# Whole-piece hi/lo splits, paired accumulator banks, and a fourth seven-product piece in every second gate-and-up loop

## The chip, the cores and the metric

The kernel runs on one core of one Trainium2 chip. The metric is the device time of one execution in microseconds (us); 1098.47 us is the median of three runs of the kernel before (1098.34 to 1099.88). Engines are named as in the profile: PE (TensorE matmul), PEld (its weight load), DVE (VectorE), ACT (ScalarE), POOL (GpSimd), SP (SyncE, which issues the weight loads).

## The reference, cut to what matters

One decoder layer on 256 tokens of width 2048, in float32. The two mixers in its first half are left out here, since the change doesn't touch them:

```python
h = _rms(x, norm1_g)
proj = einsum('bsd,de->bse', h, w_in)              # 2048 -> 6144
...                                                # gated MLP heads and retention heads
x = x + einsum('bse,ed->bsd', mixed, w_out)        # 2048 -> 2048
h2 = _rms(x, norm2_g)
a = silu(einsum('bsd,df->bsf', h2, w_gate)) * einsum('bsd,df->bsf', h2, w_up)   # 2048 -> 5632
x = x + einsum('bsf,fd->bsd', a, w_down)           # 5632 -> 2048
return _rms(x, final_norm_g)
```

## The kernel before

**Numbers.** Every operand of a product is split into a high and a low part, `hi` (a rounded copy, made by ACT in L54) and `lo` (the rest, source minus `hi`, made by DVE in L55). A product is three matmuls of 128x512 columns: hi by hi, hi by lo, lo by hi (`three`, `mm` in L46). Weights come from memory by SP in pieces of 128x2048 (`raw`, three buffers). `hi` and `lo` have four buffers each of 128x1024, so that a piece takes two of each, and a buffer comes free when the last matmul that reads it has ended.

**Stages.** `gemm_tok` runs the products with w_in (12 of them) and w_out (4); each has four pieces. Then come 11 loops over w_gu (`j` in 0 to 10, 512 columns of gate and 512 of up in each) and two halves over w_down (`c` in 0 and 1, 22 pieces each). These last two stages are written by `quad`.

**Pieces of `quad`.** A w_gu loop has 8 pieces, 0 to 7. One piece is a 2x2 product of blocks: token halves by inner halves, and inner halves by column halves. A *classic* piece makes its 8 block products in 24 matmuls. A *seven* makes them in seven products, 21 matmuls, by Strassen's way with fewer sums (Winograd's form): DVE first makes four sums of weight blocks in a tile `t` (L499, 128x1024, and L502 and L503, 128x512 each), and splits three stretches of `raw` as well as the four of `t`. `SEVEN_GU = (1, 3, 5)` says which pieces are sevens in each loop; in w_down these are 2, 6, 10, 14 and 17.

**Accumulators.** PSUM has four banks of `acc` for the results 11, 12, 21 and 22 and four of `sm`, which a quad uses for products 1, 5, 7 and 6. After the last seven of a quad ACT copies product 1 (L549) and DVE makes four mixes of the others (L550 to L553). These stand in a tile `mT2` or `mT3` until `finish_up`, where after the last piece DVE adds each of the four acc banks to its mix (L599, L600, 128x512, twice each), ACT makes silu (`sg`, L604) and DVE the product (L605), for each token half. The next loop's first matmuls reuse the acc banks that these adds read. `turn_a` transposes the product of loop j by 8 PE transposes (L615) in loop j+1, ahead of its piece 6, and ACT copies them out (L616).

**Order.** Each engine works through its own queue in the order in which the built program has it, and nothing overtakes. That order is set by a scheduler at build time, from the program's text and its buffers; it is shown below where it matters.

**The end.** In the second half over w_down the last two pieces are kept (`apart`) and run bank by bank: 11, 12, 21, 22, 12 matmuls each. DVE adds each bank to `x` in two steps of 256 columns (L684), ACT sums the squares (L226), a chain of small DVE steps makes the row's norm (L91 to L79), and DVE and ACT scale the row (L697, L700, L702) before it is stored.

## Time and profile before

| | |
|---|---|
| median of three runs | 1098.47 us |
| profiled execution | 1098.69 us |
| its span, first to last instruction | 1096.9 us |
| mean granted TensorE clock | 0.996 |
| PE busy | 1081.2 us, 99% of the span |
| PEld busy | 894.3 us, 82% |
| DVE busy | 863.4 us, 79% |
| ACT busy | 602.3 us, 55% |
| POOL busy | 26.2 us, 2% |

The share is busy time over the span. "Start us" in a timeline is counted from the span's start; the second number is how long one record, or a run of neighbours (x2, x3), took. Two instructions of one engine that follow each other overlap a little in the records, so the pace of an engine is read from one start to the next, and not from the recorded length.

### The profile page before, as it was taken

The page shows a single profiled execution, that of the slowest core. Times are in us where ns is not written, and L with a number is a line of the kernel's source. Part 1 is how long each engine was busy: PE and PEld are TensorE (multiplying, and loading weights), DVE is VectorE, ACT ScalarE, POOL GpSimd, SP SyncE. Part 2 cuts the span into 40 slices and gives each one's busy share as a digit, 9 for nine tenths or more (in the row PEclk, how much of TensorE's full clock was granted, in tenths as well). Part 3 has the DMA queues.
Part 4 walks back from the last instruction along what each step waited for, and adds up shares of the span by engine and source line. Part 5 has one row for each costly group of instructions (what it writes and reads, how often), then busy time and mean ns, then how long its engine had stood idle before and what let it go on. Part 6 is the DMA issues. An engine that isn't in the chain of part 4 may idle for free.

```text
span 1096.9 us, 12958 instructions
## 1 busy us (share of the span) xinstructions
PE 1081.2 (99%) x4907; PEld 894.3 (82%) x4907; DVE 863.4 (79%) x1149; ACT 602.3 (55%) x744; POOL 26.2 (2%) x20
## 2 busy tenths in 40 slices
PE   8999999999999999999999999999999999999996
PEld 7878888888888888888888888888888888888884
DVE  6786457466546799898898898898899887998786
ACT  6563435444445556555555655656566656565463
POOL 0110011000000000000000000000000000020000
PEclk9999999999999999999999999999999999999998
DMA  9855544445555455645655555556556655646552
GB/s 344 340 211 194 189 171 170 176 156 189 192 192 187 164 186 192 230 172 189 220 187 192 206 196 213 192 192 220 173 191 222 231 192 192 215 169 230 192 192 77
DMA packets 32750, 217.65 MB, mean 198 GB/s; under 512 B 3760, under 2 KB 4144, under 8 KB 7088
## 3 DMA queue, kind: packets, MB, share of 16 engines
q1 hardware_dynamic: 32544, 215.78, 54.9%
q0 software_dynamic: 144, 1.05, 0.3%
q8 instruction: 38, 0.62, 0.2%
q14 instruction: 24, 0.20, 0.1%
HBM read 214.72 MB, written 2.10 MB: 198 GB/s over the span
## 4 chain that ended last, share of the span: by engine, by line
PE 97%; DVE 1%; DMA 1%; ACT 0%; SPq 0%; issue 0%; DVEq 0%; ACTq 0%
PE acc L46 83%; PE sm L46 12%; PE sm L615 1%; DMA raw<-in_w_in 1%; PE sm L454 0%; PE sm L346 0%; PE sm L395 0%; DVE x L697 0%; ACT junk L226 0%; DVE x L684 0%; SPq L176 0%; DVE rs_w L78 0%; DVE st L258 0%; ACT hi L54 0%; SPq L173 0%
## 5 line engine op out<-in xcount | busy, mean ns | idle before, releaser
L46 PE MATMUL acc<-hi,hT 128*128 128x512 f32 x2364 | 752.1, 391 | 3.4 <-ACT hi L54 3.4
L54 ACT CAST hi<-raw 128x1024 fp32r<-128x1024 f32 (+1 forms) x396 | 387.9, 997 | 385.5 <-PE acc L46 358.8
L55 DVE TENSOR_TENSOR lo<-raw,hi 128x1024 fp32r<-128x1024 f32 (+1 forms) x396 | 453.0, 1161 | 181.3 <-ACT hi L54 180.0
L46 PEld LDWEIGHTS acc<-hi,hT 128*128 128x128 f32 x2364 | 443.8, 188 | 95.8 <-ACT hi L54 5.0
L46 PE MATMUL acc<-lo,hT 128*128 128x512 f32 x1182 | 460.8, 390 | 0.7 <-DVE lo L55 0.7
L46 PEld LDWEIGHTS acc<-lo,hT 128*128 128x128 f32 x1182 | 222.0, 188 | 48.3 <-DVE lo L55 3.6
L55 DVE TENSOR_TENSOR lo<-mT,hi 128x1024 fp32r<-128x1024 f32 x86 | 105.0, 1221 | 24.5 <-ACT hi L54 24.5
L54 ACT CAST hi<-mT 128x1024 fp32r<-128x1024 f32 x86 | 90.7, 1055 | 40.9 <-DVE lo L55 21.4
L46 PE MATMUL sm<-hi,h2s 128*128 128x512 f32 x258 | 93.5, 389 | 0.0
L46 PE MATMUL acc<-hi,mT 128*128 128x512 f32 x256 | 80.1, 391 | 0.0
L46 PEld LDWEIGHTS sm<-hi,h2s 128*128 128x128 f32 x258 | 48.4, 188 | 10.0
L46 PEld LDWEIGHTS acc<-hi,mT 128*128 128x128 f32 x256 | 48.1, 188 | 10.3 <-ACT mT L398 0.5
L499 DVE TENSOR_TENSOR mT<-raw 128x1024 f32<-128x1024 f32 x43 | 52.5, 1220 | 1.3 <-DMA raw<-in_w_gu 0.6
L46 PE MATMUL sm<-lo,h2s 128*128 128x512 f32 x129 | 50.2, 389 | 0.0
L46 PE MATMUL acc<-lo,mT 128*128 128x512 f32 x128 | 49.7, 389 | 0.0
L46 PE MATMUL sm<-hi,hT 128*128 128x512 f32 x86 | 33.5, 389 | 0.0
L46 PE MATMUL acc<-hi,h2s 128*128 128x512 f32 x86 | 33.5, 389 | 0.0
L502 DVE TENSOR_TENSOR mT<-raw,mT 128x512 f32<-128x512 f32 x43 | 30.6, 711 | 0.0
L604 ACT ACTIVATE sg<-mT,rstd 128x512 f32<-128x512 f32 x22 | 15.9, 722 | 24.7 <-DVE mT L599 24.7
L503 DVE TENSOR_TENSOR mT<-raw,mT 128x512 f32<-128x512 f32 x43 | 29.4, 684 | 0.0
L46 PEld LDWEIGHTS sm<-lo,h2s 128*128 128x128 f32 x129 | 24.2, 188 | 5.0
L46 PEld LDWEIGHTS acc<-lo,mT 128*128 128x128 f32 x128 | 24.0, 188 | 4.8
(111 smaller groups left out, 564.5 us busy)
## 6 DMA issues: line engine op xcount, KB each, us to landing
raw<-in_w_gu SPq DMA_DIRECT2D x88, 1024.0 KB, 4.7
raw<-in_w_in SPq DMA_DIRECT2D x47, 1024.0 KB, 4.8
raw<-in_w_down SPq DMA_DIRECT2D x44, 1024.0 KB, 4.7
raw<-in_w_out SPq DMA_DIRECT2D x16, 1024.0 KB, 4.7
x<-in_x SPq DMA_DIRECT2D x2, 1024.0 KB, 8.8
gains<-in_gains SPq DMA_DIRECT2D x2, 1024.0 KB, 6.2
out<-x SPq DMA_DIRECT2D x8, 256.0 KB, 2.5
work<-in_xT SPq DMA_DIRECT2D x7, 256.0 KB, 8.7
```

What stands on the lines that cost most here:

```text
L46: nc.tensor.matmul(o, lhsT=l, rhs=r, start=start, stop=stop)
L54: nc.scalar.copy(hi, src[:, c:c + step])
L55: nc.vector.tensor_tensor(out=lo, in0=src[:, c:c + step], in1=hi.bitcast(F32), op=ALU.subtract)
L499: nc.vector.tensor_tensor(out=t13.rearrange("p (b c) -> p b c", b=2), in0=b12.unsqueeze(1).broadcast_to([P, 2, NC]), in1=raw[:, NC:3 * NC] ...
L502: nc.vector.tensor_tensor(out=t24[:, 0:NC], in0=b22, in1=t13[:, 0:NC], op=ALU.subtract)
L503: nc.vector.tensor_tensor(out=t24[:, NC:], in0=b21, in1=t24[:, 0:NC], op=ALU.subtract)
L604: nc.scalar.activation(sg, g, AF.Silu, scale=rstd2[r])
L615: nc.tensor.transpose(ps[:, q * S + n * P:q * S + (n + 1) * P], rows[n][:, f * P:(f + 1) * P], ident)
```

## The change

1. `hi` and `lo`: three buffers of 128x2048 instead of four of 128x1024. A classic piece of `quad` is split by one ACT copy and one DVE subtraction of 2048 columns (new lines L53 and L54), where there were two of 1024. A seven's splits become two, 1536 columns of `raw` and 2048 of `t`, where there were four. `gemm_tok` still splits in steps of 1024, now into halves of one buffer.
2. `acc`: two tiles of two banks each (11 with 12, 21 with 22). `finish_up` adds a pair in one instruction of 1024 columns (L605, two in a loop, for the four L599 and L600). A pair is free for the next quad when its one add has read it.
3. Sevens of w_gu: pieces 0, 2, 4 and 6 in loops with odd `j` (five loops), 2, 4 and 6 in loops with even `j` (six). The last seven is now piece 6, so that the mixes (L555 to L558) stand after piece 6, and one classic piece is left behind it; it was piece 5, with two behind it. Products run in the order 1, 3, 2, 5, 7, 6, 4.
4. `turn_a` stands ahead of piece 7 (was 6); in loop 0 the last turn of x and the norm stand ahead of piece 1 (was 5).
5. The scratch tiles `sums` and `hf` now share the two buffers of `sg`; the load of the final gains `gf` moves from POOL's queue to SP's, in the first half over w_down.

```diff
-SEVEN_GU = (1, 3, 5)
+SEVEN_GU = (0, 2, 4, 6)
...
-    acc = ctx.enter_context(tc.tile_pool(name="acc", bufs=4, space=PSUM))
+    acc = ctx.enter_context(tc.tile_pool(name="acc", bufs=2, space=PSUM))
...
+    def pair_of_parts():
+        return [wp.tile([P, 2048], F32R, name=n, bufs=3) for n in ("hi", "lo")]
+
+    def split_into(src, hi, lo):
+
+        nc.scalar.copy(hi, src)
+        nc.vector.tensor_tensor(out=lo, in0=src, in1=hi.bitcast(F32), op=ALU.subtract)
+
     def split(src, cols, step):
-        parts = []
-        for c in range(0, cols, step):
-            hi = wp.tile([P, step], F32R, name="hi", bufs=4, padded_shape=[P, 1024])
-            lo = wp.tile([P, step], F32R, name="lo", bufs=4, padded_shape=[P, 1024])
-            nc.scalar.copy(hi, src[:, c:c + step])
-            nc.vector.tensor_tensor(out=lo, in0=src[:, c:c + step], in1=hi.bitcast(F32), op=ALU.subtract)
-            parts.append((hi, lo))
+        hi, lo = pair_of_parts()
+        parts = [(hi[:, c:c + step], lo[:, c:c + step]) for c in range(0, cols, step)]
+        for c, part in zip(range(0, cols, step), parts):
+            split_into(src[:, c:c + step], *part)
         return parts
...
-        (plain,) = split(raw[:, NC:3 * NC], 2 * NC, 2 * NC)
+        ((hi, lo),) = split(raw[:, NC:], 3 * NC, 3 * NC)
...
-        (one,) = split(t13, 2 * NC, 2 * NC)
-        (last,) = split(b21, NC, NC)
-        (two,) = split(t24, 2 * NC, 2 * NC)
+        ((thi, tlo),) = split(t, 4 * NC, 4 * NC)
...
-        bank = {k: acc.tile([P, NC], F32, name="acc") for k in ("11", "12", "21", "22")}
+        bank = {k: acc.tile([P, 2, NC], F32, name="acc") for k in "12"}
+        bank.update({k + c: bank[k][:, int(c) - 1, :] for k in "12" for c in "12"})
...
-                for k in (1, 3, 5, 7, 2, 6, 4) if i else (1, 5, 7, 6, 3, 2, 4):
+                for k in (1, 3, 2, 5, 7, 6, 4):
...
-                nc.vector.tensor_tensor(out=gs, in0=g, in1=gs, op=ALU.add)
-                nc.vector.tensor_tensor(out=us, in0=u, in1=us, op=ALU.add)
+                both = mixed[f"{r + 1}"]
+                nc.vector.tensor_tensor(out=both, in0=bank[f"{r + 1}"], in1=both, op=ALU.add)
...
         if j == 0:
-            todo[5] = [lambda: turn_x(3), norm2]
+            todo[1] = [lambda: turn_x(3), norm2]
         else:
-            todo[6] = [waiting]
-        bank, mixed = quad(lambda p: a["w_gu"][j, p], range(KD // 2), SEVEN_GU, h2_left, h2_forms, todo)
+            todo[7] = [waiting]
+        bank, mixed = quad(lambda p: a["w_gu"][j, p], range(KD // 2), SEVEN_GU[1 - j % 2:], h2_left, h2_forms, todo)
...
-    nc.gpsimd.dma_start(gf, a["gf"].partition_broadcast(P))
...
-        todo = {1: [waiting]} if c == 0 else {}
+        todo = {1: [waiting], 5: [lambda: nc.sync.dma_start(gf, a["gf"].partition_broadcast(P))]} if c == 0 else {}
```

DVE's queue at the end of loop j=1, kernel before. `lo_3790` is the second half of piece 6, `lo_3820` and `lo_3824` are piece 7, `mT0_3905` is the tile `t` of the next loop's piece 1, `lo_3872` and `lo_3876` are the next loop's piece 0:

```order
L550 TENSOR_TENSOR mT3_3765<-sm_3533,mT3_3765 128x512
L55 TENSOR_TENSOR lo_3820<-raw_3817,hi_3819 128x1024
L551 TENSOR_TENSOR mT3_3765<-sm_3531,mT3_3765 128x512
L55 TENSOR_TENSOR lo_3824<-raw_3817,hi_3823 128x1024
L552 TENSOR_TENSOR mT3_3765<-sm_3532,mT3_3765 128x512
L553 TENSOR_TENSOR mT3_3765<-sm_3532,mT3_3765 128x512
L499 TENSOR_TENSOR mT0_3905<-raw_3903 128x1024
L55 TENSOR_TENSOR lo_3872<-raw_3869,hi_3871 128x1024
L502 TENSOR_TENSOR mT0_3905<-raw_3903,mT0_3905 128x512
L55 TENSOR_TENSOR lo_3876<-raw_3869,hi_3875 128x1024
L599 TENSOR_TENSOR mT3_3765<-acc_3526,mT3_3765 128x512
L600 TENSOR_TENSOR mT3_3765<-acc_3527,mT3_3765 128x512
```

The same place in the changed kernel. `lo_3594` is piece 7, `lo_3638` and `lo_3668` are pieces 0 and 1 of the next loop (both classic, j=2), and `acc_3337` and `acc_3338` are the two pairs of loop j=1:

```order
L54 TENSOR_TENSOR lo_3594<-raw_3591,hi_3593 128x2048
L555 TENSOR_TENSOR mT3_3573<-sm_3342,mT3_3573 128x512
L54 TENSOR_TENSOR lo_3638<-raw_3635,hi_3637 128x2048
L556 TENSOR_TENSOR mT3_3573<-sm_3340,mT3_3573 128x512
L54 TENSOR_TENSOR lo_3668<-raw_3665,hi_3667 128x2048
L557 TENSOR_TENSOR mT3_3573<-sm_3341,mT3_3573 128x512
L558 TENSOR_TENSOR mT3_3573<-sm_3341,mT3_3573 128x512
L605 TENSOR_TENSOR mT3_3573<-acc_3337,mT3_3573 128x1024
L605 TENSOR_TENSOR mT3_3573<-acc_3338,mT3_3573 128x1024
```

The adds that free the accumulators now have two whole pieces of the next loop ahead of them, 2048 columns each; before it was one piece.

DVE's queue at the end of loop j=2, kernel before; the next loop's piece 0 (`lo_4207`, `lo_4211`) is classic and its piece 1 (`lo_4242` and what follows) is a seven:

```order
L553 TENSOR_TENSOR mT2_4100<-sm_3867,mT2_4100 128x512
L441 TENSOR_TENSOR sums_6970<-af1_3125 128x128
L499 TENSOR_TENSOR mT1_4240<-raw_4238 128x1024
L55 TENSOR_TENSOR lo_4207<-raw_4204,hi_4206 128x1024
L55 TENSOR_TENSOR lo_4211<-raw_4204,hi_4210 128x1024
L599 TENSOR_TENSOR mT2_4100<-acc_3861,mT2_4100 128x512
L600 TENSOR_TENSOR mT2_4100<-acc_3862,mT2_4100 128x512
L502 TENSOR_TENSOR mT1_4240<-raw_4238,mT1_4240 128x512
L605 SCALAR_TENSOR_TENSOR mT2_4100<-mT2_4100,rstd2_0_3349,sg_4188 128x512
L599 TENSOR_TENSOR mT2_4100<-acc_3863,mT2_4100 128x512
L600 TENSOR_TENSOR mT2_4100<-acc_3864,mT2_4100 128x512
L55 TENSOR_TENSOR lo_4242<-raw_4238,hi_4241 128x1024
```

The same place in the changed kernel; the next loop (j=3) starts with a seven, whose splits are `lo_3926` (raw) and `lo_3933` (`t`), and `lo_3960` is its classic piece 1:

```order
L555 TENSOR_TENSOR mT2_3860<-sm_3634,mT2_3860 128x512
L54 TENSOR_TENSOR lo_3926<-raw_3922,hi_3925 128x1536
L556 TENSOR_TENSOR mT2_3860<-sm_3632,mT2_3860 128x512
L54 TENSOR_TENSOR lo_3933<-mT0_3924,hi_3932 128x2048
L557 TENSOR_TENSOR mT2_3860<-sm_3633,mT2_3860 128x512
L558 TENSOR_TENSOR mT2_3860<-sm_3633,mT2_3860 128x512
L605 TENSOR_TENSOR mT2_3860<-acc_3629,mT2_3860 128x1024
L605 TENSOR_TENSOR mT2_3860<-acc_3630,mT2_3860 128x1024
L505 TENSOR_TENSOR mT1_3989<-raw_3987 128x1024
L610 SCALAR_TENSOR_TENSOR mT2_3860<-mT2_3860,rstd2_0_3048,sg_3909 128x512
L610 SCALAR_TENSOR_TENSOR mT2_3860<-mT2_3860,rstd2_1_3073,sg_3913 128x512
L54 TENSOR_TENSOR lo_3960<-raw_3957,hi_3959 128x2048
```

The split of piece 1 now stands behind both adds, the first sum of piece 2's `t` (L505) and both products L610. On PE the first matmuls of piece 1 are two that need only its `hi`, then one of piece 2, then one that needs `lo_3960`.

DVE's queue at the end of the program, kernel before (`x0` and `x1` are the token halves, `acc_7804` is bank 21, `acc_7805` is 22):

```order
L78 TENSOR_SCALAR rs_w_8725<-rs_r_8722,rs_h_8719 128x1
L684 TENSOR_TENSOR x1_73<-acc_7804,x1_73 128x256 x2
L79 TENSOR_SCALAR rs_r_8726<-rs_w_8725,rs_r_8722 128x1
L78 TENSOR_SCALAR rs_w_8729<-rs_r_8726,rs_h_8719 128x1
L79 TENSOR_SCALAR rs_r_8730<-rs_w_8729,rs_r_8726 128x1
L697 SCALAR_TENSOR_TENSOR x0_72<-x0_72,rs_r_8730,hT3_6876 128x512 x2
L684 TENSOR_TENSOR x1_73<-acc_7805,x1_73 128x256 x2
```

And in the changed kernel, where `acc_7049` is the pair of 21 and 22, and a row of the first half (`x0`, pair `acc_7048`, x4) stands before this stretch, ahead of its norm:

```order
L82 TENSOR_SCALAR rs_w_7861<-rs_r_7858,rs_h_7855 128x1
L83 TENSOR_SCALAR rs_r_7862<-rs_w_7861,rs_r_7858 128x1
L82 TENSOR_SCALAR rs_w_7865<-rs_r_7862,rs_h_7855 128x1
L83 TENSOR_SCALAR rs_r_7866<-rs_w_7865,rs_r_7862 128x1
L701 SCALAR_TENSOR_TENSOR x0_72<-x0_72,rs_r_7866,hT3_6232 128x512 x2
L688 TENSOR_TENSOR x1_73<-acc_7049,x1_73 128x256 x4
```

The four adds of `x1` now stand together behind all that is done for `x0`; before, two of them stood in the middle of it.

## Rows read from the trace of the kernel before

**Rows 1.** The page: engines' busy time and share, and DVE's tenths in 40 slices.

```profile
PE 1081.2 (99%) x4907; PEld 894.3 (82%) x4907; DVE 863.4 (79%) x1149; ACT 602.3 (55%) x744; POOL 26.2 (2%) x20
...
DVE  6786457466546799898898898898899887998786
```

**Rows 2.** Windows of the w_gu and w_down stages; columns: window, length, busy time by engine, clock, DMA.

```profile
560.00:640.00 80.00, 80.00 (x362) 66.05 (x361) 69.24 (x77) 46.47 (x52) 0.00 (x0) 1.00 0.58 203
...
850.00:1070.00 220.00, 219.98 (x974) 181.26 (x973) 185.03 (x213) 128.98 (x152) 7.96 (x5) 1.00 0.55 201
```

**Rows 3.** The chain that ended last, in order of time; columns: start, length, what.

```profile
606.85 6.12 PE acc L46 x27
...
629.55 15.69 PE acc L46 x69
...
672.02 15.69 PE acc L46 x69
```

**Rows 4.** DVE's timeline at a loop's end; columns: start, length, engine and line, tiles, shape.

```profile
614.10 1.23 DVE L55 TENSOR_TENSOR lo<-mT,hi 128x1024 fp32r<-128x1024 f32 x1
615.24 0.69 DVE L502 TENSOR_TENSOR mT<-raw,mT 128x512 f32<-128x512 f32 x1
615.84 3.49 DVE L55 TENSOR_TENSOR lo<-raw,hi 128x1024 fp32r<-128x1024 f32 x3
...
628.15 0.69 DVE L550 TENSOR_TENSOR mT<-sm,mT 128x512 f32<-128x512 f32 x1
628.76 1.22 DVE L55 TENSOR_TENSOR lo<-raw,hi 128x1024 fp32r<-128x1024 f32 x1
...
632.22 0.68 DVE L553 TENSOR_TENSOR mT<-sm,mT 128x512 f32<-128x512 f32 x1
...
637.21 0.68 DVE L599 TENSOR_TENSOR mT<-acc,mT 128x512 f32<-128x512 f32 x1
...
639.01 0.74 DVE L605 SCALAR_TENSOR_TENSOR mT<-mT,rstd,sg 128x512 f32<-128x512 f32 x1
639.67 0.68 DVE L599 TENSOR_TENSOR mT<-acc,mT 128x512 f32<-128x512 f32 x1
```

**Rows 5.** ACT's timeline at the same loop's end.

```profile
624.21 0.58 ACT L549 COPY mT<-sm 128x512 f32<-128x512 f32 x1
...
625.92 3.10 ACT L54 CAST hi<-raw 128x1024 fp32r<-128x1024 f32 x3 [0.19 <-PE sm L46]
...
639.89 1.05 ACT L54 CAST hi<-mT 128x1024 fp32r<-128x1024 f32 x1 [0.30 <-PE acc L46]
```

**Rows 6.** PE's timeline at the same loop's end.

```profile
627.77 0.60 PE L615 MATMUL sm<-ident,mT 128*128 128x128 f32 x4
...
628.91 0.64 PE L615 MATMUL sm<-ident,mT 128*128 128x128 f32 x4
...
639.41 0.62 PE L46 MATMUL acc<-hi,hT 128*128 128x512 f32 x2
```

**Rows 7.** All engines' timeline at the end of the program.

```profile
1077.74 0.19 PEld L46 LDWEIGHTS acc<-lo,hT 128*128 128x128 f32 x1 [0.33 <-DVE lo L55]
...
1081.06 0.76 DVE L684 TENSOR_TENSOR x<-acc,x 128x256 f32<-128x256 f32 x2 [1.78 <-PE acc L46]
...
1081.86 0.42 ACT L226 ACTIVATE junk<-x 128x256 bf16<-128x256 f32 x1 [1.83 <-DVE x L684]
...
1082.40 0.42 ACT L226 ACTIVATE junk<-x 128x256 bf16<-128x256 f32 x1
...
1082.94 0.21 DVE L94 TENSOR_SCALAR rs_u<-sq,rs_v 128x1 f32<-128x1 f32 x1 [0.19 <-ACT junk L226]
...
1084.32 0.75 DVE L684 TENSOR_TENSOR x<-acc,x 128x256 f32<-128x256 f32 x2
...
1085.78 1.41 DVE L697 SCALAR_TENSOR_TENSOR x<-x,rs_r,hT 128x512 f32<-128x512 f32 x2
...
1087.11 0.75 DVE L684 TENSOR_TENSOR x<-acc,x 128x256 f32<-128x256 f32 x2
```

More of the change, by code (lines that the diff above doesn't have):

```diff
@@ L28 @@
 EPS = 1e-6
-PAD_BIG = 480
+PAD_BIG = 224
 PAD_BASE = 16
-SEVEN_GU = (1, 3, 5)
+SEVEN_GU = (0, 2, 4, 6)
 SEVEN_DOWN = (2, 6, 10, 14, 17)
@@ L111, in gemm_tok @@
     def gemm_tok(lT, pieces, order, todo=(), apart=0):
-        ps = [acc.tile([P, NC], F32, name="acc") for _ in range(NT)]
+        ps = acc.tile([P, NT, NC], F32, name="acc")
+        ps = [ps[:, n, :] for n in range(NT)]
         todo = dict(todo)
@@ L179, in block_kernel @@
         if g == 0:
-            first += split(raw[:, 0:NC], NC, NC)
+            hi0, lo0 = pair_of_parts()
+            first.append([(hi0[:, c:c + NC], lo0[:, c:c + NC]) for c in range(0, 2048, NC)])
+            split_into(raw[:, 0:NC], *first[0][0])
         for q in range(4):
@@ L188, in block_kernel @@
             if g == 0 and q < 3:
-                first += split(raw[:, (q + 1) * NC:(q + 2) * NC], NC, NC)
+                split_into(raw[:, (q + 1) * NC:(q + 2) * NC], *first[0][q + 1])
         if g > 0:
             first.append(split(raw, 2048, NC if g == 1 else 1024))
-    first = [first[0:4]] + first[4:]
     csn = mix.tile([P, NT, 2, 64], F32, name="csn")
@@ L438, in sums_of @@
     def sums_of(x11, x12, x21, x22, dst):
-        t = ff.tile([P, 4, P], F32, name="sums", bufs=1)
+        t = ff.tile([P, 4, P], F32, name="sg", bufs=2)
         nc.vector.tensor_tensor(out=t[:, 0, :], in0=x21, in1=x22, op=ALU.add)
@@ L465, in turn_x @@
             if p in SEVEN_GU:
-                hf = ff.tile([P, 2, S], F32, name="hf", bufs=1)
+                hf = ff.tile([P, 2, S], F32, name="sg", bufs=2)
                 for j in range(2):
@@ L485, in pair_classic @@
     def pair_classic(src):
-        return load_piece(src)
+        return load_piece(src, 2048)
     odd = itertools.count()
@@ L503, in pair_seven @@
         nc.vector.tensor_tensor(out=t24[:, NC:], in0=b21, in1=t24[:, 0:NC], op=ALU.subtract)
-        (one,) = split(t13, 2 * NC, 2 * NC)
-        (last,) = split(b21, NC, NC)
-        (two,) = split(t24, 2 * NC, 2 * NC)
-        cut = lambda part, h: tuple(x[:, h * NC:(h + 1) * NC] for x in part)
-        return {1: cut(plain, 0), 3: cut(plain, 1), 5: cut(one, 0), 7: cut(one, 1),
-                6: cut(two, 0), 4: cut(two, 1), 2: cut(last, 0)}
+        ((thi, tlo),) = split(t, 4 * NC, 4 * NC)
+        cut = lambda h, l, c: (h[:, c * NC:(c + 1) * NC], l[:, c * NC:(c + 1) * NC])
+        return {1: cut(hi, lo, 0), 3: cut(hi, lo, 1), 2: cut(hi, lo, 2),
+                5: cut(thi, tlo, 0), 7: cut(thi, tlo, 1), 6: cut(thi, tlo, 2), 4: cut(thi, tlo, 3)}
     def three(bank, left, right, start, stop):
@@ L547, in quad @@
                     t = big.tile([P, 4, NC], F32, name=f"mT{2 + next(odd_quad) % 2}")
-                    t1, v, w, z = (t[:, i, :] for i in range(4))
+                    t1, w, v, z = (t[:, i, :] for i in range(4))
                     nc.scalar.copy(t1, bank[1])
@@ L553, in quad @@
                     nc.vector.tensor_tensor(out=v, in0=bank[7], in1=v, op=ALU.add)
-                    mixed = {"11": t1, "12": w, "21": v, "22": z}
+                    mixed = {"11": t1, "12": w, "21": v, "22": z, "1": t[:, 0:2, :], "2": t[:, 2:4, :]}
                 continue
-            (h0, l0), (h1, l1) = pair_classic(src(p))
-            cut = lambda h, l, c: (h[:, c * NC:(c + 1) * NC], l[:, c * NC:(c + 1) * NC])
-            right = {"12": cut(h0, l0, 0), "11": cut(h0, l0, 1), "22": cut(h1, l1, 0), "21": cut(h1, l1, 1)}
+            ((hi, lo),) = pair_classic(src(p))
+            right = {
+                k: (hi[:, c * NC:(c + 1) * NC], lo[:, c * NC:(c + 1) * NC]) for c, k in enumerate(("12", "11", "22", "21"))}
             todo_rows = [(p, right, i == len(order) - 1)]
@@ L784 @@
     }
-    nc = bacc.Bacc("TRN2", target_bir_lowering=False, num_devices=1)
+    nc = bacc.Bacc("TRN2", target_bir_lowering=False, num_devices=1, dynamic_dma_scratch_size=1024)
     feeds, args = {}, {}
```

## The prediction

> **What bounds the kernel now.** I read the page's shares first: PE is busy 99% of the span, DVE 79%, in the right half of its tenths 8 to 9 in most slices [rows 1]. Then the windows: in 80 us of the w_gu loops PE is busy all 80 us, at full granted clock, while DVE is busy 69.24; over w_down it is 219.98 of 220 against 185.03 [rows 2]. Then the chain in order of time, which in these stages is matmuls alone: 27 of them take 6.12 us, 0.2267 each, and a w_gu loop lasts from 629.55 to 672.02, 42.47 us, for 183 matmuls (41.5) and eight transposes [rows 3]. So the kernel is as long as its matmuls, and any matmul saved counts in full so long as nothing else becomes late. What could become late is DVE, which makes every `lo`. The question is thus one of order: at which places does DVE's queue, with its new and longer instructions, deliver later than PE asks?
>
> **What is saved.** Five loops have a fourth seven, each with 3 matmuls fewer: 15 x 0.2267 = **-3.40 us**. The w_down half keeps its pieces.
>
> **Prices.** DVE's pace is read from start to start [rows 4]: 1024 columns 1.14 (614.10 to 615.24; three in 3.41), 512 columns 0.60, the product 0.66 (639.01 to 639.67). A line through 0.60 and 1.14 gives 1.66 for 1536 columns and 2.2 for 2048. That line is an estimate, as no instruction in the trace is that wide. So the wide splits save DVE only some 0.07 us an instruction. In columns, a fourth seven costs DVE a wide sum, two half sums and 1536 more columns of split, 4 us (1.14 + 2 x 0.60 + 1.66). By order rows and these paces a loop with three sevens needs some 35.6 us of DVE and one with four 39.6, against 41.8 of PE. On average there is room; the places decide. ACT: 1024 columns 1.00 (three in 3.01), the copy L549 0.47 to the next start, 2048 hence about 1.9 [rows 5]. A buffer freed by PE starts ACT's copy some 0.25 us after PE goes on (639.41 is two matmuls, the second at 639.64, the copy at 639.89) [rows 5, 6]. DVE's result reaches PE 0.06 us after its recorded end [rows 7], which is 0.08 past its pace; I add 0.14. Transposes: 0.36 and 0.40 by start to start, 0.8 in all [rows 6].
>
> **Piece by piece inside a loop.** A seven and a classic piece take PE 21 + 24 matmuls, 4.76 + 5.44 = 10.2 us, and DVE 2.2 (classic) + 1.66 + 2.2 (the seven's splits) + 2.34 (its sums) = 8.4. The classic piece's buffer comes free as the seven starts: 0.25, ACT 1.9, DVE 2.2, done at 4.4, needed at 4.76 + 0.23. It just holds; I count nothing, and 0 to 0.3 for each of some 30 such pairs as the bound.
>
> **A loop of four into one of three** (after j = 1, 3, 5, 7, 9; first place in the order rows). Time 0 is the start of piece 6, a seven. Piece 7's buffer is freed then: ACT 0.25 to 2.2, its `lo` 2.24 to 4.44. Next L555 to 5.04, the next loop's piece 0 to 7.24 (its `hi` is ready by 4.8), L556 to 7.84, piece 1 to 10.04, L557 and L558 to 11.24, and only then the add of the first pair, to 12.38, seen by PE at 12.5. PE has done piece 6 at 4.76, the transposes at 5.56, piece 7 at 11.0, and its next matmul writes that pair. It waits 1.5 us. Before, this add stood behind one piece of the next loop and ran at 637.21, 2.2 us ahead of 639.41 [rows 4, 6], when the loop ended: two classic pieces came after the mixes. Five times: **+7.5**. Bounds 0.8 and 2.0 each, from 2048 columns at 2.0 and at two of 1.14.
>
> **A loop of three into one of four** (after j = 2, 4, 6, 8; second place). The same up to L555 at 5.04; then 1.66 to 6.7, L556 7.3, 2.2 to 9.5, L557 and L558 10.7, the two adds 11.84 and 12.98, L505 14.1, two products 15.4, and the `lo` of piece 1 to 17.6, seen at 17.75. ACT is not later: it copies `hi` of piece 1 from 11.25 to 13.15, then two `sg`. PE has its first seven done at 11.0 + 4.76 and three more matmuls that need no `lo` of piece 1, at 16.45. It waits 1.3. Four times: **+5.2**; bounds 0.5 and 2.0. After j=0 there are no transposes (PE is 0.8 earlier) and the split stands ahead of one product: the pair is missed by 0.9 and the split by little, **+1.0**.
>
> **The other places.** Loop 10 into w_down: as the first kind, with one split of 1024 columns (L652) in place of piece 1; late by **0.5**. First half of w_down into the second: the split of the second piece, done 4.4 after the last piece's start, stands ahead of the four adds of the pair (4 x 0.38 [rows 7]), 5.9 + 0.1 against 5.44: **+0.5**. Loop 0: the norm's chains now stand between splits at piece 1, one chain is 2.84 less the 0.66 of adds inside it [rows 7]; 0 to 1.5, I take **+0.5**, since the splits ahead have a piece in hand. The load of `gf` on SP's queue: its wait, for the end of loop 10, stands ahead of a load for w_down's fifth piece, four pieces before its use; DMA share is 0.55 [rows 2]: nothing. The products with w_in and w_out keep their split of 1024, but hold three pieces instead of two, and a buffer comes free only with its whole piece: 0, between -0.5 and +0.5.
>
> **The end.** The first half's pair is whole when its second bank was before, at the release of 1081.06. Four adds follow, not two, so four sums of squares, 0.54 apart (1081.86, 1082.40), run from 1081.56 to 1083.7; the chain starts at 1083.75, not 1082.94, takes 2.84 less the 0.66 of the two adds that no longer stand in it, and its two L701 end at 1087.3. The last half's adds start there, not at 1087.11: +0.2; and four sums of squares follow instead of two, +1.1 [rows 7]. **+1.3.**
>
> **Sum.** 1098.69 - 3.40 + 7.5 + 5.2 + 1.0 + 0.5 + 0.5 + 0.5 + 1.3 = 1111.8; the profiled run is 0.2 over the median, so **1111.6 us**.
>
> **A rule beside it.** DVE is 79% busy [rows 1], not saturated. The Trainium skill, "Perfetto Trace Analysis", section "Optimizing Scalar/DVE Operations", says that grouping into larger operations helps where the engine is saturated, and that where it isn't, but makes bubbles on others, breaking instructions up may let work complete sooner. The first would give the faster rival below; the second speaks against 2048 columns. By rows 1 and 2 the second is the one that applies.
>
> **Rivals.** *Faster: the queue is not late.* If 2048 columns took DVE 1.7 rather than 2.2, three of them would give back the 1.5 us of the first kind, and the second kind nearly so. What remains is the matmuls and the end: 1098.5 - 3.4 + 1.3 = 1096.4. For it: DVE's load fits on average, and PE never waited in these stages. Against it: the pace is straight between 512 and 1024 columns. It lies just at the bound of what is called faster, so the chance of 0.20 goes 0.13 to faster and 0.07 to same (the end at 0.9 or at 1.7 decides). *Half of it:* only one kind of loop end costs, since a step in my walk is earlier than I have it: 1096.4 + 7.5 + 1 = 1105, or 1103 with the other; 1099 to 1107, chance 0.13. *Worse:* the inner pairs are late too, 0.3 x 30 = 9, 1121; DVE at 39.6 of 41.8 leaves no time to catch up. Chance 0.07. Forecast, 1107 to 1117: 0.60.
>
> **The numbers.** Two runs of this kernel can be told apart at about 0.2%, 2.2 us. Faster, below 1096.3, holds 0.13 of the first rival; within 0.2% the rest of it and a little of the second, 0.08; slower the rest, 0.79. The range takes in the half of the first rival that lies above its own time, and leaves out the other half and the third, 0.17: 1096.4 to 1117.
>
> **What would show it.** PE waits of 1.3 to 1.6 us at the first matmul of loops 2, 4, 6, 8 and 10 on the add L605, of about as much in piece 1 of loops 3, 5, 7 and 9 on L54; DVE's wide `lo` at 2.2 from start to start; PE's busy time 3.4 lower. Were these waits missing and DVE's queue idle ahead of the adds, my walk would be wrong; waits inside the loops would be the third rival.

## The result, and the profile of the changed kernel

The changed kernel takes **1112.49 us** (median of four runs, 1111.07 to 1113.72) against 1098.40 for the kernel before on the same chip: a ratio of 1.0121, 95% interval 1.0109 to 1.0134. The prediction was 1111.6 us, slower than before. The profiled execution spans 1111.2 us at a granted clock of 0.995, 14.3 more than the 1096.9 of before.

**The page.** The line of busy times, against [rows 1] and the table of before:

```profile
PE 1084.0 (98%) x4892; PEld 892.7 (80%) x4892; DVE 868.2 (78%) x977; ACT 574.5 (52%) x577; POOL 23.9 (2%) x19
```

DVE's share hardly moves, 79% to 78%. By shares nothing happened, and yet the kernel is 14 us longer. (PE's busy time even rose by 2.8, with 15 matmuls fewer. A matmul's record lasts 0.39 and its pace, from start to start, is 0.227, so the first 0.16 of each gap counts as busy; and where the granted clock falls, below, each record is longer.)

**What PE waited for.** The view of PE's waits names it. Columns: engine, what waits, its line, releaser, then us in total, times, longest:

```profile
PE acc L46 <- DVE mT L605: 6.5, 6, 1.3
PE acc L46 <- DVE lo L54: 4.1, 5, 1.0
PE acc L46 <- ACT hi L53: 1.6, 2, 1.0
```

L605 is the add of a pair of accumulator banks, L54 the split. The first row is five loop ends of 1.3 and one of 0.2, the second mostly four of 0.9 to 1.0. (A wait's number is about 0.15 less than the gap that it makes between two starts, for the same reason. Below I give gaps: the time from one matmul's start to the next, less the pace of 0.2267.)

**First place, a loop of four sevens into one of three.** DVE at the end of loop j=1, then the first matmul of loop j=2:

```profile
463.25 0.68 DVE L555 TENSOR_TENSOR mT<-sm,mT 128x512 f32<-128x512 f32 x1
463.85 2.28 DVE L54 TENSOR_TENSOR lo<-raw,hi 128x2048 fp32r<-128x2048 f32 x1
466.05 0.69 DVE L556 TENSOR_TENSOR mT<-sm,mT 128x512 f32<-128x512 f32 x1
466.64 2.28 DVE L54 TENSOR_TENSOR lo<-raw,hi 128x2048 fp32r<-128x2048 f32 x1
468.85 0.69 DVE L557 TENSOR_TENSOR mT<-sm,mT 128x512 f32<-128x512 f32 x1
469.44 0.68 DVE L558 TENSOR_TENSOR mT<-sm,mT 128x512 f32<-128x512 f32 x1
470.04 2.35 DVE L605 TENSOR_TENSOR mT<-acc,mT 128x1024 f32<-128x1024 f32 x2
```

```profile
471.41 0.47 PE L46 MATMUL acc<-hi,hT 128*128 128x512 f32 x1 [1.30 <-DVE mT L605]
```

DVE has no idle time here: it works through two splits of the next loop, at 463.85 and 466.64, and PE waits for the add behind them. A row like it stands at 558.94, 646.67, 733.97 and 822.06. The gap is 1.40 to 1.46 each time.

**Second place, three into four**, DVE and then PE in piece 1 of loop j=3:

```profile
513.39 2.35 DVE L605 TENSOR_TENSOR mT<-acc,mT 128x1024 f32<-128x1024 f32 x2
515.65 1.22 DVE L505 TENSOR_TENSOR mT<-raw 128x1024 f32<-128x1024 f32 x1
516.78 1.41 DVE L610 SCALAR_TENSOR_TENSOR mT<-mT,rstd,sg 128x512 f32<-128x512 f32 x2
518.11 3.96 DVE L54 TENSOR_TENSOR lo<-raw,hi 128x2048 fp32r<-128x2048 f32 x2
```

```profile
520.45 0.50 PE L46 MATMUL acc<-lo,hT 128*128 128x512 f32 x1 [0.97 <-DVE lo L54]
```

The gap is 1.10 to 1.14, four times (also at 608.34, 695.72, 783.83). The queue ahead of the split is the one of the order rows: adds, a sum, two products.

**Third place, loop j=1**, where PE stood longer than I had it. DVE, ACT, PE, and two windows (columns: busy us and count of PE, PEld, DVE, ACT, POOL, then granted clock, DMA share, GB/s):

```profile
435.63 1.23 DVE L505 TENSOR_TENSOR mT<-raw 128x1024 f32<-128x1024 f32 x1 [1.28 <-DMA raw<-in_w_gu]
436.89 0.69 DVE L508 TENSOR_TENSOR mT<-raw,mT 128x512 f32<-128x512 f32 x1
437.50 2.29 DVE L54 TENSOR_TENSOR lo<-mT,hi 128x2048 fp32r<-128x2048 f32 x1
```

```profile
434.47 1.92 ACT L53 CAST hi<-mT 128x2048 fp32r<-128x2048 f32 x1 [5.63 <-DVE mT L509]
```

```profile
438.24 0.49 PE L46 MATMUL acc<-hi,hT 128*128 128x512 f32 x1 [0.61 <-ACT hi L53]
439.84 0.50 PE L46 MATMUL sm<-lo,h2s 128*128 128x512 f32 x1 [1.11 <-DVE lo L54]
441.08 0.63 PE L46 MATMUL sm<-lo,h2s 128*128 128x512 f32 x1
441.51 0.63 PE L46 MATMUL sm<-hi,h2s 128*128 128x512 f32 x1
```

```profile
440.00:442.00 2.00, 2.00 (x7) 1.56 (x8) 2.00 (x2) 0.00 (x0) 0.00 (x0) 0.66 0.00 0
442.00:444.00 2.00, 2.00 (x6) 1.58 (x5) 2.00 (x2) 0.00 (x0) 0.00 (x0) 0.50 0.40 82
```

This is piece 2 of the loop, a seven. ACT could copy its `t` only at 434.47, when DVE had made the sums. Then, at 435.63, DVE waited 1.28 for a transfer: the sums of piece 4 had been put ahead of the split of piece 2's `t`, and piece 4's weights had not landed. PE lost 0.77 and then 1.37, and then the granted clock fell to 0.50, the lower of its two levels (1.2 GHz): matmuls start 0.43 apart, not 0.227, from 440.66 to 444.07, 1.6 us more.

**The end.** The last matmul, and DVE's last four adds of a pair into `x`:

```profile
1098.99 0.39 PE L46 MATMUL acc<-hi,hT 128*128 128x512 f32 x1
1100.24 1.41 DVE L688 TENSOR_TENSOR x<-acc,x 128x256 f32<-128x256 f32 x4
```

From the last matmul's start to the end of the span it is 12.21 us, before 1096.9 - 1086.07 = 10.83. Four adds in a row stand where there were two [rows 7].

**Where 14.3 us came from**, by the starts of the same matmuls in both traces: up to the transposes of x at 346.92 (350.32 before) -3.4; loop 0 to j=1 +3.7 (4.4 of lost time, less three matmuls saved); the nine loops from there to j=10 +12.4 (the 12 matmuls saved there in it, so some 15 us of waits); loop 10 into w_down +0.3; both halves of w_down 0.0; the end +1.4.

### The profile page after: what moved, and what is told of

The parts are those of the page before. It is cut to its first block, busy times and chain, and to the rows that moved or that the text cites. A ratio compares the mean times of both kernels' runs of the same rounds, so it can differ in the third digit from the quotient of the medians.

```text
span 1111.2 us, 12366 instructions
## 1 busy us (share of the span) xinstructions
PE 1084.0 (98%) x4892; PEld 892.7 (80%) x4892; DVE 868.2 (78%) x977; ACT 574.5 (52%) x577; POOL 23.9 (2%) x19
## 4 chain that ended last, share of the span: by engine, by line
PE 78%; DVE 13%; issue 3%; ACT 3%; DMA 2%; SPq 0%; DVEq 0%; ACTq 0%
PE acc L46 69%; PE sm L46 8%; DVE lo L54 7%; ACT hi L53 3%; DVE mT L605 1%; DMA raw<-in_w_gu 1%; DVE mT L505 1%; DMA raw<-in_w_in 1%; DVE mT L556 1%; DVE mT L557 1%; DVE mT L610 1%; DVE mT L555 0%; ACT junk L232 0%; PE sm L460 0%; PE sm L352 0%
## 5 line engine op out<-in xcount | busy, mean ns | idle before, releaser
L46 PE MATMUL acc<-hi,hT 128*128 128x512 f32 x2304 | 735.0, 391 | 8.4 <-DVE mT L605 6.5
L54 DVE TENSOR_TENSOR lo<-raw,hi 128x1024 fp32r<-128x1024 f32 (+3 forms) x264 | 430.5, 1655 | 127.3 <-ACT hi L53 126.4
L53 ACT CAST hi<-raw 128x1024 fp32r<-128x1024 f32 (+3 forms) x264 | 361.4, 1393 | 315.7 <-PE acc L46 269.6
L46 PEld LDWEIGHTS acc<-hi,hT 128*128 128x128 f32 x2304 | 433.3, 188 | 101.5 <-issue 8.8
L46 PE MATMUL acc<-lo,hT 128*128 128x512 f32 x1152 | 450.0, 391 | 4.2 <-DVE lo L54 4.1
L53 ACT CAST hi<-mT 128x2048 fp32r<-128x2048 f32 x48 | 92.0, 1916 | 154.8 <-DVE mT L509 111.5
L54 DVE TENSOR_TENSOR lo<-mT,hi 128x2048 fp32r<-128x2048 f32 x48 | 110.0, 2292 | 52.3 <-ACT hi L53 52.3
L505 DVE TENSOR_TENSOR mT<-raw 128x1024 f32<-128x1024 f32 x48 | 58.2, 1222 | 7.2 <-DMA raw<-in_w_gu 5.0
L46 PE MATMUL sm<-lo,h2s 128*128 128x512 f32 x144 | 57.4, 399 | 1.1 <-DVE lo L54 1.1
L509 DVE TENSOR_TENSOR mT<-raw,mT 128x512 f32<-128x512 f32 x48 | 32.7, 690 | 1.0
L508 DVE TENSOR_TENSOR mT<-raw,mT 128x512 f32<-128x512 f32 x48 | 32.7, 690 | 0.8
L652 DVE TENSOR_TENSOR hT<-af,hT 128x1024 fp32r<-128x1024 f32 x22 | 26.8, 1219 | 0.0
```

Source lines behind the costliest of these rows:

```text
L46: nc.tensor.matmul(o, lhsT=l, rhs=r, start=start, stop=stop)
L53: nc.scalar.copy(hi, src)
L54: nc.vector.tensor_tensor(out=lo, in0=src, in1=hi.bitcast(F32), op=ALU.subtract)
L505: nc.vector.tensor_tensor(out=t13.rearrange("p (b c) -> p b c", b=2), in0=b12.unsqueeze(1).broadcast_to([P, 2, NC]), in1=raw[:, NC:3 * NC] ...
L508: nc.vector.tensor_tensor(out=t24[:, 0:NC], in0=b22, in1=t13[:, 0:NC], op=ALU.subtract)
L509: nc.vector.tensor_tensor(out=t24[:, NC:], in0=b21, in1=t24[:, 0:NC], op=ALU.subtract)
```

## The experiments

My theory: the waits come from the **order** of DVE's queue at loop ends, what stands ahead of an add or a split. The rivals: DVE's **load** with four sevens, the **width** of its instructions, or **buffers**. Ratios are to the kernel before, run beside each on the same chip; the runs stand on several chips, on which the kernel before has medians from 1098.01 to 1098.68. Line numbers shift from run to run.

### The whole change but the sevens

```diff
-SEVEN_GU = (0, 2, 4, 6)
+SEVEN_GU = (1, 3, 5)
...
-        bank, mixed = quad(lambda p: a["w_gu"][j, p], range(KD // 2), SEVEN_GU[1 - j % 2:], h2_left, h2_forms, todo)
+        bank, mixed = quad(lambda p: a["w_gu"][j, p], range(KD // 2), SEVEN_GU, h2_left, h2_forms, todo)
```

> The changed kernel with sevens 1, 3 and 5 in all eleven loops, as before the change (15 sevens fewer, 45 matmuls more: +10.2 us against... 15 pieces x 3 matmuls x 0.2267 = +3.4 us); all else as changed, the wide splits and the paired banks too. Theory 'queue at the loop's end' (the mixes stand behind piece 6, with one classic piece left, and two whole splits of the next loop go ahead of the adds): with the last seven at 5 the adds have two classic pieces of cover, the waits on L605 and in piece 1 go, about 1097 us (1095 to 1099.5). Rival 'wide splits and paired banks make PE wait by themselves': the waits at the loop's end stay, 1106 or more. Rival 'the fourth seven fills DVE': also about 1097, so that this run alone does not tell it from the theory; the next one does.

Measured 1097.55, ratio 0.9984 (0.9975 to 0.9994). No wait on L605 or of over 0.4 on L54 is left in the w_gu loops. So wide splits and paired banks alone cost nothing there, and width as such is out; what is lost hangs on where the sevens stand or on how many there are. The next run tells these apart.

### Three sevens in every loop, at the new places

```diff
-        bank, mixed = quad(lambda p: a["w_gu"][j, p], range(KD // 2), SEVEN_GU[1 - j % 2:], h2_left, h2_forms, todo)
+        bank, mixed = quad(lambda p: a["w_gu"][j, p], range(KD // 2), SEVEN_GU[1:], h2_left, h2_forms, todo)
```

> The changed kernel with sevens 2, 4 and 6 in all eleven loops: no loop has a fourth seven, but the last seven stays at piece 6. Theory 'queue at the loop's end': all ten loop ends are now of the first kind, so ten waits of about 1.4 us on L605 instead of five, none of about 1.1 in piece 1, 3.4 us of matmuls more: 1109 to 1113 us. Rival 'the fourth seven fills DVE': the waits go with it, 1096 to 1099 us.

Measured 1114.48, ratio 1.0135 (1.0117 to 1.0152). The waits:

```profile
PE acc L46 <- DVE mT L605: 12.6, 10, 1.3
```

Ten loop ends, ten waits of the first kind, 1.42 each in gaps, with not one fourth seven in the program, and DVE has less to do than in the changed kernel. Load is out for this kind: it comes with one classic piece behind the mixes in place of two. The time came out 1.5 above the top of what I expected; a wait of 1.56 on ACT at 426.12, near the start of loop 1, and matmuls at half pace behind it, as in the third place above, are the likely rest:

```profile
428.00:430.00 2.00, 2.00 (x6) 1.61 (x5) 2.00 (x3) 0.46 (x1) 0.00 (x0) 0.50 0.15 61
```

### A fourth seven between the old ones

```diff
-SEVEN_GU = (0, 2, 4, 6)
+SEVEN_GU = (1, 2, 3, 5)
...
-        bank, mixed = quad(lambda p: a["w_gu"][j, p], range(KD // 2), SEVEN_GU[1 - j % 2:], h2_left, h2_forms, todo)
+        bank, mixed = quad(lambda p: a["w_gu"][j, p], range(KD // 2), (SEVEN_GU if j % 2 else (1, 3, 5)), h2_left, h2_forms, todo)
```

> The changed kernel with sevens 1, 2, 3 and 5 in loops with odd j and 1, 3 and 5 in those with even j: as many matmuls as the changed kernel, the same DVE load in total, but the last seven at piece 5 and piece 0 classic in every loop. Theory 'queue at the loop's end': almost no waits, about 1094 us (1092 to 1098); three sevens in a row may be late by some tenths. Rival 'the fourth seven fills DVE' (39.6 of 41.8 us in such a loop): the waits move into the loop, 1104 or more.

Measured 1111.09, ratio 1.0102 (1.0077 to 1.0127): a clear miss, and the time that I had written for the rival (1104 or more). PE, then ACT and DVE, in loop j=3, then the windows behind these waits in j=3 and behind the same in j=5:

```profile
529.20 0.98 PE L46 MATMUL sm<-hi,h2s 128*128 128x512 f32 x3 [1.20 <-ACT hi L53]
531.00 0.50 PE L46 MATMUL acc<-hi,hT 128*128 128x512 f32 x1 [0.59 <-ACT hi L53]
```

```profile
527.24 1.91 ACT L53 CAST hi<-mT 128x2048 fp32r<-128x2048 f32 x1 [4.53 <-DVE mT L509]
```

```profile
519.70 1.22 DVE L505 TENSOR_TENSOR mT<-raw 128x1024 f32<-128x1024 f32 x1
520.84 2.29 DVE L54 TENSOR_TENSOR lo<-mT,hi 128x2048 fp32r<-128x2048 f32 x1
523.04 1.75 DVE L54 TENSOR_TENSOR lo<-raw,hi 128x1536 fp32r<-128x1536 f32 x1
524.71 0.69 DVE L508 TENSOR_TENSOR mT<-raw,mT 128x512 f32<-128x512 f32 x1
525.31 1.22 DVE L505 TENSOR_TENSOR mT<-raw 128x1024 f32<-128x1024 f32 x1
526.45 0.68 DVE L509 TENSOR_TENSOR mT<-raw,mT 128x512 f32<-128x512 f32 x1
```

```profile
532.00:534.00 2.00, 2.00 (x7) 1.52 (x6) 2.00 (x2) 0.33 (x1) 0.00 (x0) 0.50 0.02 4
620.00:622.00 2.00, 2.00 (x9) 1.65 (x10) 2.00 (x2) 0.72 (x1) 0.00 (x0) 1.00 0.00 0
```

I had looked at the loop's end alone. Here three sevens stand next to each other, and DVE has no idle time from 515.72 to 528.46. The sums of the third seven's `t` (519.70, 524.71, 526.45) have two splits and a sum for a later piece between them, so that ACT's copy at 527.24 waits 4.53 for the last. By the prediction's prices a seven takes DVE 6.2 us and PE 4.76, a classic piece 2.2 and 5.44: three sevens in a row put DVE behind, in a loop whose average has room. So this loss is DVE's load in one stretch, as the rival said; the order in that stretch adds to it, and no run tells the two apart here. The clock fell to 0.50 behind these waits too, in j=3 and j=9, but not behind waits of the same lengths in j=5. Inside a loop, too, a seven needs a classic piece beside it.

### The kernel before with only the wide buffers and splits

```diff
-            hi = wp.tile([P, step], F32R, name="hi", bufs=4, padded_shape=[P, 1024])
-            lo = wp.tile([P, step], F32R, name="lo", bufs=4, padded_shape=[P, 1024])
...
+        return [wp.tile([P, 2048], F32R, name=n, bufs=3) for n in ("hi", "lo")]
...
-        return load_piece(src)
+        return load_piece(src, 2048)
```

> The kernel before with one part of the change: three hi and lo buffers of 2048 columns and whole-piece splits (and, to find the room, the scratch tiles shared with sg and the load of gf on SP's queue); sevens, accumulator banks and the order of products as before. The changed kernel reaches the first transposes of x 3.4 us earlier than the kernel before. Theory: that gain is from these buffers (a piece more is split ahead), so about 1095 us (1094 to 1097) and no waits in the loops. Rival: it comes from another part of the change, 1098.4 us; second rival, wide splits are late in the loops: 1100 or more.

Measured **1095.18**, ratio 0.9962 (0.9949 to 0.9975): faster than both kernels. (The edit also shares the scratch tiles and moves the load of `gf`, to find the room.) The largest part of the gain is one wait of the kernel before, in the products with w_in, which no trace with three wide buffers has:

```profile
59.99 0.72 PE L46 MATMUL acc<-hi,hT 128*128 128x512 f32 x2 [1.59 <-ACT hi L54]
```

Its gap is 1.75. The rest are small ones: 0.8 in w_down, 0.04 in most loops of w_gu; one gap of 0.77 in loop j=1 goes the other way. (Of the -3.4 above the other part lies in the first 20 us, which vary: in the changed kernel and the runs made from it the first transposes of x start between 346.8 and 349.1, against 350.3 before.) These buffers, which hold a piece more ahead, are worth some 3 us, and the changed kernel gave it away again.

### The same instructions in another order, first step

```diff
+            with tc.issue_after(first_add[-1]) if i == 1 and first_add else ExitStack():
+                ((hi, lo),) = pair_classic(src(p))
...
+        with tc.issue_after(added.ins) if mixed else ExitStack():
+            for r, (t, u, sg) in enumerate(last_of):
+                nc.vector.scalar_tensor_tensor(out=t, in0=u, scalar=rstd2[r], in1=sg, op0=ALU.mult, op1=ALU.mult)
...
+        with tc.issue_after(last_t[-1]) if behind else ExitStack():
+            nc.vector.tensor_tensor(
+                out=t13.rearrange("p (b c) -> p b c", b=2), in0=b12.unsqueeze(1).broadcast_to([P, 2, NC]),
+                in1=raw[:, NC:3 * NC].rearrange("p (b c) -> p b c", b=2), op=ALU.subtract)
```

> The changed kernel with the same instructions, in another order in DVE's queue at the loop ends only: the split of a loop's piece 1 stands behind the previous loop's first pair add (L605 of the changed kernel), both products L610 stand behind the second add in the loops that end here, and the sums of piece 4 of a four-seven loop stand behind the split of t of piece 2. Theory (order alone makes the waits; the changed kernel runs at 1112.5): the five waits of 1.42 on L605 go (-7.1), the four of 1.1 on L54 and the small ones around them go for the most part (-4.5 to -7), and the place in j=1 with its lower clock goes in part (-2 to -4): 1096 to 1100, with no group 'acc <- DVE mT L605' of over 1 us in all. Rival (DVE's load with four sevens, or the width of its instructions, makes PE wait, in whatever order): the waits move to inner pieces and the time stays at 1108 or more.

Measured 1105.96, ratio 1.0063 (1.0050 to 1.0077): 6.5 better than the changed kernel, and 6 short of what I expected. The waits on the adds are gone (one of 0.2 is left), as they should be. But two loops still take 2.05 more than their matmuls and transposes need. DVE in loop j=3, then PE (L55 is here ACT's copy, L56 the split, L508 the first sum, L622 the product):

```profile
515.05 2.29 DVE L56 TENSOR_TENSOR lo<-raw,hi 128x2048 fp32r<-128x2048 f32 x1 [0.30 <-ACT hi L55]
517.26 1.41 DVE L622 SCALAR_TENSOR_TENSOR mT<-mT,rstd,sg 128x512 f32<-128x512 f32 x2
518.59 1.75 DVE L56 TENSOR_TENSOR lo<-raw,hi 128x1536 fp32r<-128x1536 f32 x1
520.26 1.22 DVE L508 TENSOR_TENSOR mT<-raw 128x1024 f32<-128x1024 f32 x1
...
524.98 2.29 DVE L56 TENSOR_TENSOR lo<-mT,hi 128x2048 fp32r<-128x2048 f32 x1 [2.05 <-ACT hi L55]
```

```profile
526.81 0.49 PE L46 MATMUL acc<-hi,hT 128*128 128x512 f32 x1 [0.57 <-ACT hi L55]
```

The split of piece 1 comes in time now. The next seven, piece 2, does not: its sums begin at 520.26, behind the products and the split of `raw`; then ACT copies `t`, and DVE stands idle for 2.05 until that is done. It is a chain, sums on DVE, copy on ACT, split on DVE, and it was started too late. PE loses 0.74, 0.29 and 0.11 here, 0.11, 0.29 and 0.11 in piece 4, and 0.1 or so in each of a few more. The rival had said that waits would move to inner pieces, and in part they did: by this run alone, load and order can't be told apart for the second kind.

### The same order, and single banks over w_down

```diff
+        if one_pool:
+            bank = {k: one_pool[0].tile([P, NC], F32, name="one") for k in ("11", "12", "21", "22")}
```

> The run with the new order in DVE's queue, and the accumulators of the two halves over w_down in four single banks as in the kernel before; w_gu keeps its pairs. Theory (the pairs cost 1.38 at the end of the program, and 0.5 at the boundary of the two halves over w_down): 1.4 to 1.9 below the run with the order alone, so 1094 to 1098, and the last matmul to end of span 10.8 instead of 12.2. Rival (the end's 1.38 comes from the wide splits or another place): equal to the run with the order alone within 0.5.

Measured 1105.04, ratio 1.0060 (1.0047 to 1.0073), 0.9 below the run before it; I had expected 1.4 to 1.9, and 1094 to 1098 in all, since I counted on the first step. The two times can't be told apart (1.0063, 1.0050 to 1.0077, before), so what the banks cost is read from the traces. The end is as expected: from the last matmul (1092.39) to the end of the span (1103.0) 10.6 us, against 1105.9 - 1093.79 = 12.1 with pairs. So the pairs make the end's 1.4. But where pairs turn into single banks, at loop 10 into w_down, a new wait came in (L615 is here the add of a pair):

```profile
858.98 0.47 PE L47 MATMUL one<-hi,hT 128*128 128x512 f32 x1 [1.41 <-DVE mT L615]
```

Its gap is 1.57, against 0.35 there with pairs. By the traces -1.5 - 0.5 (the boundary of the halves, where no gap is left) + 1.2 = -0.8.

### Classic pieces split in halves again

```diff
-        return load_piece(src, 2048)
+        return load_piece(src)
```

> The changed kernel with the classic pieces of w_gu and w_down split in two steps of 1024 again, inside the same buffers of 2048; sevens keep their wide splits, pairs and sevens stay. The order that the scheduler then makes has both adds ahead of the split of piece 1 at loop ends, but in loops before a four-seven loop the split of t of piece 0 behind the adds. Theory (what stands in DVE's queue ahead of what, not the width): the five waits of 1.42 on L605 go (-7.1), the other four loop ends wait 2 to 3 on L54 instead of 1.1 (+4 to +8), DVE carries 0.07 more for each classic piece: 1107 to 1112. Rival (smaller instructions let work complete sooner at every place): both kinds go, 1099 to 1102. Rival (more DVE time per loop): slower than the changed kernel, above 1113.

Measured 1112.90, ratio 1.0129 (1.0115 to 1.0143): no better than the changed kernel, 0.9 above what I expected and just under what the second rival said, so that the time decides nothing; the waits do. With halves the scheduler makes another order: the adds are in time at every loop end, and the split of `t` of piece 0 is late instead. The waits:

```profile
PE sm L46 <- DVE lo L54: 5.3, 4, 2.2
PE sm L46 <- ACT hi L53: 5.0, 5, 1.8
```

The group of L605 is gone. Instead PE waits on hi and lo of `t`, in gaps up to 2.36, and in two places the clock falls behind them (0.54 at 616 to 618, 0.50 at 696 to 698). The Trainium skill, "Perfetto Trace Analysis", section "Optimizing Scalar/DVE Operations", says that where an engine isn't saturated but causes bubbles on others, breaking up instructions may let work complete sooner. At the adds it did: 6.5 us of waits on L605 became none. But the new order put other work late, and the time stayed.

### The kernel before with wide splits and the new sevens, on single banks

```diff
-SEVEN_GU = (1, 3, 5)
+SEVEN_GU = (0, 2, 4, 6)
...
-        bank, mixed = quad(lambda p: a["w_gu"][j, p], range(KD // 2), SEVEN_GU, h2_left, h2_forms, todo)
+        bank, mixed = quad(lambda p: a["w_gu"][j, p], range(KD // 2), SEVEN_GU[1 - j % 2:], h2_left, h2_forms, todo)
```

(with the turns and the product order of the change)

> The kernel before with the wide buffers and wide splits of whole pieces, and with the sevens, turns and product order of the change, but with single banks and so four adds of 512 columns at a loop's end. Against the run with the buffers alone (1095.2) it adds the sevens. Theory (order): the scheduler's order has the adds ahead of the split of piece 1, so the loops of four into three don't wait; the split of t of piece 0 stands behind the adds, so the loops of three into four wait 3 to 5 on L54, four times, and j=1 too: 1095.2 - 3.4 + 12 to 20, 1104 to 1111, no waits of over 0.5 on the adds at the first matmul of loops 2, 4, 6, 8 and 10. Rival (the sevens are paid by the pairs' late release alone): 1092 to 1095.

Measured 1110.38, ratio 1.0118 (1.0093 to 1.0142), as expected. The first kind isn't there; the second is worse, since the split of piece 0's `t`, and already the last sum that it needs, stand behind the adds:

```profile
514.92 0.97 PE L46 MATMUL sm<-hi,h2s 128*128 128x512 f32 x3 [1.98 <-ACT hi L53]
```

Behind the same waits in the next three loops of four the clock fell as well, which is part of the time. So the change's two parts meet in one place: whole splits and pairs with one classic piece behind the mixes make the first kind, and with single banks the order that comes out makes the second kind larger. The releaser was ACT's hi of `t`, not L54 as I had written; it is the same chain of sums, copy and split as in the run with halves.

### The same instructions in another order, second step

```diff
+        if sums_first:
+            with tc.issue_after(summed.ins):
+                ((hi, lo),) = split(raw[:, NC:], 3 * NC, 3 * NC)
...
-                right = pair_seven(src(p), p == 4 and 0 in seven)
+                right = pair_seven(src(p), p == 4 and 0 in seven, p == 2 and 0 in seven)
...
+        if j % 2 or j == NF - 1:
+            products(lambda: added.ins)
+        else:
+            later.append(lambda: products(lambda: last_t[-1]))
...
-        todo = {}
+        todo = {3: [later.pop()]} if later else {}
```

> The run with the new order in DVE's queue (1106.0), and two more moves of the same instructions there, only in loops of four sevens: the two products of the loop before stand behind the split of t of piece 2 (ahead of them until now), and in piece 2 the three sums of t stand ahead of the split of raw. In the run with the first new order each loop of four still lost 2.05 (0.74 at a matmul of piece 2 that waited for ACT's hi of t, 0.29 behind it, 0.44 in piece 4, and three of 0.1), since t was made only at 522.9 and DVE then idled 2.05 until its hi was there. By the queue's rows and paces t is now whole some 3 us earlier and its lo done at 524.0 in place of 527.2. Theory (order and the chain sums, hi, lo): 1.5 to 2.0 less in each of five loops, 1096 to 1099. Rival (DVE has too much to do at the start of a loop of four, in whatever order): the waits move to another piece and the time stays at 1104 or more.

Measured **1097.68**, ratio 0.9991 (0.9982 to 1.0000): 8.3 less than the first step, within the 1096 to 1099 that order alone should give, and 14.8 less than the changed kernel with the same work (4892 matmuls and 977 DVE instructions in both; by the ratios 7.9 and 14.3). DVE at the same place (L56 is the split, L509 the first sum, L627 the product):

```profile
512.53 2.29 DVE L56 TENSOR_TENSOR lo<-raw,hi 128x2048 fp32r<-128x2048 f32 x1 [0.28 <-ACT hi L55]
514.74 1.22 DVE L509 TENSOR_TENSOR mT<-raw 128x1024 f32<-128x1024 f32 x1
...
517.33 1.75 DVE L56 TENSOR_TENSOR lo<-raw,hi 128x1536 fp32r<-128x1536 f32 x1
519.46 2.29 DVE L56 TENSOR_TENSOR lo<-mT,hi 128x2048 fp32r<-128x2048 f32 x1 [0.39 <-ACT hi L55]
521.67 1.41 DVE L627 SCALAR_TENSOR_TENSOR mT<-mT,rstd,sg 128x512 f32<-128x512 f32 x2
```

The sums come right behind the split of piece 1, the split of `raw` fills the time in which ACT copies `t` (the idle time is 0.39, was 2.05), and the products, which nobody needs before piece 7, stand last. Of the 2.05 per loop of four some 0.5 are left.

### The first step without the products

```diff
+        if j % 2 == 0 and j < NF - 1:
+            return [sg for _, _, sg in last_of]
```

> The run with the new order in DVE's queue (1106.0), with the two products at the end of the loops with even j (0 to 8) left out: the transposes take ACT's silu in place of the product, so the gate isn't multiplied by the other half in these loops. DVE has 1.33 less to do in each, right ahead of piece 2's split; nothing else is changed. If DVE's load there makes PE wait: t and its lo come some 1.5 earlier, 1.1 to 2.0 less in each of five loops, 1096 to 1101. Rival (the wait for ACT's hi comes from ACT or from a buffer): within 1 of 1106.

Measured 1098.83, ratio 0.9998 (0.9988 to 1.0007), as expected. Taking 1.33 of DVE's work away ahead of the chain does nearly what moving it does. So both readings hold for the second kind: DVE is tight there, and that is why the order decides.

## Why the prediction held, point by point

**The frame** held: PE's matmuls are the length, so every wait at a loop end counts in full, and the average room on DVE (78% busy) helps nothing. The Trainium skill, "Perfetto Trace Analysis", section "Optimizing Scalar/DVE Operations", has one rule for grouping work where an engine is saturated and one for breaking it up where it isn't but makes bubbles. Neither gave the time, which was 1112.5 with whole splits and 1112.9 with halves.

**DVE's pace** was the first disputed number, since the trace of before had no instruction so wide. 128x2048 runs from 463.85 to 466.05, 2.20 from start to start, as the line gave it; 1536 columns take 1.67 (506.74 to 508.41 in the first run with a new order), where the line said 1.66. The rival that hung on 1.7 fell with it. ACT's copy of 2048 columns takes 1.81 from start to start (434.47 to 436.28; 1.92 recorded), where I had about 1.9.

**First kind:** 5 x 1.5 predicted, 1.40 to 1.46 each measured, 7.1 in place of 7.5. **Second kind:** 4 x 1.3 predicted, 1.10 to 1.14 measured, on the releaser that I had named. But each two loops lost some 0.8 more, which I had at nothing: 0.13 to 0.19 in the later pieces of the loops of four, 0.1 behind each wait, and at 771.24 the transposes, which waited 0.50 for a bank of `sm` whose mix (L555) stood behind a split. So the walk broke off too early: it ended at piece 1, and the backlog went on to piece 4, as the first step of the new order then showed. With it the second kind is nearer to 8 than to 5.2. The third rival (inner pairs late, up to 0.3 each) was this, in small.

**Loop 0 to j=1** was the step that failed: 0.5 + 1.0 predicted, 4.4 measured, and not at the places of my walk. The norm in loop 0 (0.5) and the pair that was to be missed by 0.9 cost nothing: no gap stands at either. The split of piece 1 cost 0.34, "by little" as I had it. The rest lies in piece 2, which I hadn't walked: I took the sums of the next seven as work that hides, and here they stood ahead of a split that PE needed, with a DMA wait of 1.28 in them. And 1.6 of it is the granted clock, on which I had counted nothing.

**Early stages:** I had 0, within half a us. They gave back 1.75 at 59.99, a wait of the kernel before that I hadn't looked at, since I read only the loops; in this trace 3.4 with the start's own variation. This and j=1 cancel: -3.4 against 4.4 - 1.5 = +2.9. That the total came within 1 us is luck to that extent.

**The rest** held: loop 10 into w_down 0.32 (predicted 0.5), the boundary of the halves 0.47 (0.5, though the view names ACT's sum of squares, L232, as the releaser and not the adds), the end 1.38 (1.3), the load of the gains nothing. One sign failed: PE's busy time was to be 3.4 lower and rose by 2.8. It can't serve as a sign, since part of every gap counts as busy.

**The cause** is what stands ahead of what in DVE's queue. For the first kind that is shown: ten waits came where DVE had less to do than in the changed kernel, and they went when the same instructions were moved. For the second kind moving them is enough, and so is giving DVE 1.33 us less to do: the order decides where DVE is tight, and in the one run with three sevens in a row DVE fell behind. In all, some 14 us went with the order alone. Of the 0.5 left in a loop of four the trace has two gaps of 0.13 to 0.22, with 0.1 behind each; what makes them is not shown; at the transposes of loop j=8 it is a mix behind a DMA wait of 1.53, as in j=1.

**What the fourth seven is worth:** little, even well ordered. In the second step two loops take 588.86 - 504.06 = 84.8 us, from transposes to transposes; before it is 542.84 - 457.88 = 84.96. So 0.68 saved, 0.5 given back. The paired banks cost 1.4 at the end and 0.5 between the halves, and the run with buffers alone stays ahead by 2.5 us (3.2 by the ratios).
